# The levels of a gated linear attention: their multiplications all on VectorE, and dense projections set between their products

## The chip, the cores and the metric

The kernel runs on one core of one Trainium2 chip. Its engines work side by side, each through a queue of its own in order: TensorE (PE, matrix products into PSUM), VectorE (DVE), ScalarE (ACT), GpSimd (POOL, which works on SBUF only) and SyncE (SP), which issues the DMAs. The metric is the device time of one execution in microseconds. A shorter time is better. The kernel before takes 3704.74 us, the median of three runs (3701.15 to 3706.63).

## The reference

Two layers of a hybrid transformer over 1024 latent tokens and 256 context tokens, width 1024, in fp32. Each layer has one input projection whose columns are split among three head groups (a 2-D neighbourhood attention, a bidirectional gated linear attention, and a grouped-query attention), one output projection, and a SwiGLU feed-forward block. What the change touches is the projection of the neighbourhood attention's queries and keys, and the part of the linear attention inside its chunks of 64 tokens. The reference computes that part for one direction as

```python
b = jnp.cumsum(gi, axis=-2)
diff = b[..., :, None, :] - b[..., None, :, :]
decay = jnp.exp(jnp.where(causal[:, :, None], diff, -jnp.inf))
A = jnp.einsum('bhtd,bhsd,bhtsd->bhts', qi, ki, decay)
o = jnp.einsum('bhts,bhsv->bhtv', A, vi) + jnp.einsum('bhtd,bhdv->bhtv', qi * jnp.exp(b), S)
```

so that each pair of tokens (t, s) of a chunk has its own decay, the product of all gates between s and t, for each of 32 channels.

## The kernel before

**Layout.** Activations lie with features on the 128 partitions and tokens along the free dimension: 1280 columns, 1024 latent and 256 context. A dense projection is computed with split operands. Each fp32 value is a rounded high part and the rest as a low part, and a product is three matrix products (high x high, high x low, low x high). `mm3` issues them: 8 slices of the inner dimension x 3 = 24 products of up to 512 columns. That is one **chunk**. `wunit` fetches a weight block of 1024 x 128 (a DMA on SP, L238), casts it to its high part on ACT (whi, L249) and subtracts for the low part, here on POOL (wlo, L252). `dense` runs one such block over the token ranges (512, 512 and 256 columns in the first layer and for the keys; the second layer's queries have the two 512 only) and hands each chunk's PSUM bank to an evacuation function. `dense_g` and `products_g` are the same as generators, one chunk per step.

**The linear attention's levels.** The decays inside a chunk of 64 tokens are built in six levels, by doubling. At level `lev` two halves of w = 2^lev tokens meet. Four arrays of 128 x 1280 hold the running decay products: `Fd` and `Hd` (both called dec in the profile; they come from the gates by ACT's exponentials) and `Gd` and `Jd` (which begin as ones). At each level (L603 to L624):
- DVE multiplies the queries with Fd or Hd into X (L609, two halves), POOL the keys with Gd and Jd into xk (L610, L611);
- PE multiplies xk with X in small tiles (`a_mm`, L586: 32 rows, 64 x 64 results) into one of two PSUM buffers called aps. A call is for one of two head pairs and up to eight groups of 128 tokens. The second layer has 8 groups, so two calls a level; the first has 10, so four, two with eight groups and two with two;
- DVE copies the result under the level's mask into A (copy_predicated, L614);
- the four decay arrays are brought to the next level (L621 on DVE, L622 to L624 on POOL).

Ahead of the levels stands one more product without decay, whose diagonal goes into A (L597).

**The neighbourhood projections.** Behind the levels in program order stand six `dense` calls (L638 to L640): for each of three blocks the keys (3 chunks) and the queries (3 chunks in the first layer, 2 in the second), 18 and 15 chunks. `put` evacuates a chunk: ACT scales it into sphi (L630), DVE computes the low part splo (L631), and SP stores both (L633, L634). Behind them come the projection of the linear attention's values, the scan over its states on DVE (L735), and the other projections, woven with the output of the linear attention (L743 and on).

**What sets the order.** The order in each engine's queue is fixed when the kernel is built, by a planner that goes by program order and by its own estimate of when an instruction's operands are there. It may put a chunk between the levels' products where it expects PE to be free. `gate(ins, after)` adds an order between two instructions of one engine without a wait on the chip; `in_order` chains a list of them.

**The modulation's weights.** In the first layer the products with `w_ada` for the later parts are made on DVE (`ada_step`, L177 and L179), 64 steps of two instructions with a weight tile from a DMA each. `ada_later` queues them; every chunk calls `ada_tick(pace["steps"])`, which runs the steps whose weights were fetched at the tick before and fetches for the next ones. Every eight steps two small products with ones add up the sums (L185).

Of the kernel before, what the change touches and what calls it, by code (L numbers as in the profile page):

```python
# [9 lines left out]
F32R = mybir.dt.float32r  # L10
U32 = mybir.dt.uint32
I32 = mybir.dt.int32
AF = mybir.ActivationFunctionType
ALU = mybir.AluOpType
# [5 lines left out]
P = 128  # L20
# [12 lines left out]
FULL = ((0, 512), (512, 512), (1024, 256))  # L33
# [13 lines left out]
W_NQ, W_NK, W_NV, W_LV, W_LQ, W_LK, W_LG, W_LR, W_GQ, W_GK, NW = (  # L47
    0, 384, 768, 1280, 1536, 1664, 1792, 2048, 2080, 2464, 2592)
# [5 lines left out]
def body(ctx: ExitStack, tc, xT, cT, w_ada, w_in, nbias, wa2, w_out, w_fi, w_fo, vecs, cc, consts, ropes, gmask, out):  # L54
    nc = tc.nc
    act, dve, pool, pe = nc.scalar, nc.vector, nc.gpsimd, nc.tensor
# [3 lines left out]
    tmp = ctx.enter_context(tc.tile_pool(name="tmp", bufs=5))  # L60
# [12 lines left out]
    def slot(dt=F32, name="sl"):  # L73
        return slots.tile([P, NT], dt, tag="s", name=name)
# [4 lines left out]
    def bank_q(name):  # L79
        return ps_q.tile([P, 512], F32, tag="q", name=name)  # L80
# [7 lines left out]
    def banks2(pool_, tag, name):  # L88

        return pool_.tile([P, 2, 512], F32, tag=tag, name=name)  # L90
# [4 lines left out]
    def f(ap):  # L95
        return ap.bitcast(F32)
# [68 lines left out]
    ada_todo, ada_run, ada_st = [], [], {}  # L165
# [96 lines left out]
    def mm3(ps, wh, wl, xh, xl, t0, n, c0, cn, natural=False, ks=None):  # L262
        nk = len(xh)
        o = ps[:cn, :n]
        if natural and t0 < SEQ:

            def pick(t):
                return t[:, 0:SEQ].rearrange("p (g r c) -> p r g c", g=8, r=16)[:, t0 // 64:(t0 + n) // 64]
            o = o.rearrange("p (r g c) -> p r g c", g=8, c=8)
        else:  # L270
            def pick(t):
                return t[:, t0:t0 + n]
        for k in ks or range(nk):
            a, b = wh(k, c0, cn), wl(k, c0, cn)
            r, q = pick(xh[k]), pick(xl[k])
            for lhs, rhs, st in ((a, r, k == 0), (a, q, False), (b, r, False)):
                ins = pe.matmul(o, lhsT=lhs, rhs=rhs, start=st, stop=(k == nk - 1 and lhs is b))  # L277
                slip(ins, n, st or (ks and k == ks[0] and rhs is r and lhs is a))
        ada_st["after"] = ins
        return ins  # L280


    hooks = []
# [2 lines left out]
    def slip(ins, n, first):  # L286

        if not hooks:
            return
        if first and hk["last"] is not None:  # L290
            gate(ins, hk["last"])
        hk["c"] += n
        while hooks and hooks[0][0] <= hk["c"]:
            gate(ins, hooks.pop(0)[1])
        hk["last"] = ins if hooks else None
# [5 lines left out]
    pace = {"n": 0, "every": 1, "steps": 1, "w": 0, "lo": 0}  # L301

    def dense(src, xh, xl, tcs, evac, cols=P, natural=False):
        wh, wl = wunit(src, len(xh), cols)
        products(wh, wl, xh, xl, tcs, evac, cols, natural)
# [8 lines left out]
    def run(g):  # L314
        for _ in g:
            pass

    def products(*args):
        run(products_g(*args))

    def dense_g(src, xh, xl, tcs, evac, cols=P, natural=False):
        wh, wl = wunit(src, len(xh), cols)
        yield from products_g(wh, wl, xh, xl, tcs, evac, cols, natural)
# [110 lines left out]
    def gate(ins, after):  # L434

        if after is not None:
            tc.add_manual_dep(ins.ins, after.ins.name, NOSYNC, reason="buffers in order of use")
        return ins

    def in_order(inss):  # L440

        for a, b in zip(inss, inss[1:]):
            gate(b, a)
        return inss[-1]
# [66 lines left out]
    S_NK, S_NQ, S_GQ, S_GK = 0, 3, 6, 9  # L511
    sp = [[dram.tile([2, P, NT], F32, name=f"sp{l}_{i}") for i in range(10)] for l in range(NL)]
# [4 lines left out]
    uh = [slot(F32R, f"uh{k}") for k in range(KT)]  # L517
    ul = [slot(F32R, f"ul{k}") for k in range(KT)]
# [6 lines left out]
    for l in range(NL):  # L525
        last = l == NL - 1
        V = vec[l]
        TOK = LAT if last else FULL
        CT = ((1024, 256),)

        def win(c0, n):
            return w_in[l, :, c0:c0 + n]
# [28 lines left out]
        for e in range(2):  # L561
            ba = V[:, V_BA + e:V_BA + e + 1]
            for (t0, n) in FULL:
                ps = bank_q("zps")
# [4 lines left out]
        ins = [act.activation(a, a, AF.Exp, scale=-1.0) for a in dec][-1]  # L569
        ins = [gate(act.activation(a, a, AF.Ln, bias=one1), ins) for a in dec][-1]  # L570
# [8 lines left out]
        NG = NQ // P  # L579
# [3 lines left out]
        def a_mm(p, ga, gb, xk_, X):  # L583

            ps = banks2(ps_s, "s", "aps")
            in_order([pe.matmul(ps[64 * c:64 * c + 64, hh, (g - ga) * 64:(g - ga + 1) * 64],  # L586
                                lhsT=xk_[32 * (2 * p + hh):32 * (2 * p + hh) + 32, P * g + 64 * c:P * g + 64 * c + 64],
                                rhs=X[32 * (2 * p + hh):32 * (2 * p + hh) + 32, P * g + 64 * c:P * g + 64 * c + 64],
                                start=True, stop=True)
                      for g in range(ga, gb) for c in range(2) for hh in range(2)])  # L590
            return (A[p][:, ga:gb].rearrange("p g h t -> p h g t"),
                    ps[:, :, :(gb - ga) * 64].rearrange("p h (g t) -> p h g t", t=64), gb - ga)

        abanks = [(p, g, min(g + 8, NG)) for g in range(0, NG, 8) for p in range(2)]
        for p, ga, gb in abanks:
            dst, src, n = a_mm(p, ga, gb, gk, gq)
            dve.tensor_tensor(out=dst, in0=src, in1=diag2.unsqueeze(1).unsqueeze(1).to_broadcast([P, 2, n, 64]),  # L597
                              op=ALU.mult)

        def hv(t, n, w):  # L600
            return t[:, :n].rearrange("p (b s w) -> p b s w", s=2, w=w)

        for lev in range(6):  # L603
            w = 1 << lev
            xk_, X = slot(F32, "xk2"), slot(F32, "X")
            g4, j4 = hv(Gd, NQ, w), hv(Jd, NQ, w)
            k4, xk4, q4, X4 = hv(gk, NQ, w), hv(xk_, NQ, w), hv(gq, NQ, w), hv(X, NQ, w)
            for s, dec_ in ((1, Fd), (0, Hd)):
                dve.tensor_tensor(out=X4[:, :, s], in0=q4[:, :, s], in1=hv(dec_, NQ, w)[:, :, s], op=ALU.mult)  # L609
            pool.tensor_tensor(out=xk4[:, :, 0], in0=k4[:, :, 0], in1=g4[:, :, 0], op=ALU.mult)  # L610
            pool.tensor_tensor(out=xk4[:, :, 1], in0=k4[:, :, 1], in1=j4[:, :, 1], op=ALU.mult)  # L611
            for p, ga, gb in abanks:
                dst, src, n = a_mm(p, ga, gb, xk_, X)
                dve.copy_predicated(dst, gm[:, lev].unsqueeze(1).unsqueeze(1).to_broadcast([P, 2, n, 64]), src)  # L614
            f4, h4, g4, j4 = hv(Fd, NT, w), hv(Hd, NT, w), hv(Gd, NT, w), hv(Jd, NT, w)
            nb = NT // (2 * w)

            def bc(ap):
                return ap.to_broadcast([P, nb, w])

            dve.tensor_tensor(out=g4[:, :, 0], in0=g4[:, :, 0], in1=bc(f4[:, :, 1, w - 1:w]), op=ALU.mult)  # L621
            pool.tensor_tensor(out=j4[:, :, 1], in0=j4[:, :, 1], in1=bc(h4[:, :, 0, 0:1]), op=ALU.mult)  # L622
            pool.tensor_tensor(out=f4[:, :, 1], in0=f4[:, :, 1], in1=bc(f4[:, :, 0, w - 1:w]), op=ALU.mult)
            pool.tensor_tensor(out=h4[:, :, 0], in0=h4[:, :, 0], in1=bc(h4[:, :, 1, 0:1]), op=ALU.mult)  # L624


        def put(i, t0, n, src, scale=1.0):
            hi = tmp.tile([P, 512], F32R, tag="t5", name="sphi")
            lo = tmp.tile([P, 512], F32R, tag="t5", name="splo")
            act.activation(hi[:, :n], src, AF.Copy, scale=scale)  # L630
            dve.scalar_tensor_tensor(out=lo[:, :n], in0=src, scalar=scale, in1=f(hi[:, :n]),  # L631
                                     op0=ALU.mult, op1=ALU.subtract)
            nc.sync.dma_start(sp[l][i][0, :, t0:t0 + n], f(hi[:, :n]))  # L633
            nc.sync.dma_start(sp[l][i][1, :, t0:t0 + n], f(lo[:, :n]))  # L634

        if l == 0:
            ada_later(0, (2, 4, 3, 5))
        for i in range(3):  # L638
            dense(win(W_NK + i * P, P), uh, ul, FULL, lambda ps, t0, n, _, i=i: put(S_NK + i, t0, n, ps[:, :n], 0.125))
            dense(win(W_NQ + i * P, P), uh, ul, TOK, lambda ps, t0, n, _, i=i: put(S_NQ + i, t0, n, ps[:, :n]))  # L640

        def v_unit(c0, dst):

# [57 lines left out]
        for p in range(2):  # L701
# [28 lines left out]
            for i in range(1, NCH - 1):  # L730
                for e in range(2):
                    c, nx = order[e][i], order[e][i + 1]
# [3 lines left out]
                                             op0=ALU.mult, op1=ALU.add)  # L736
# [389 lines left out]
        for x, i in enumerate(PAIRS):  # L1126
# [12 lines left out]
            n = done = 0  # L1139
# [42 lines left out]
        first = [(m, w, t0, n, bank_q("mmps")) for m, w in enumerate(wo) for i, (t0, n) in enumerate(LAT)]  # L1182
# [36 lines left out]
        for nh in HCH:  # L1219
            hs = [(slot(F32R, "hh"), slot(F32R, "hl")) for _ in range(nh)]  # L1220
            hh, hl = [h_[0] for h_ in hs], [h_[1] for h_ in hs]
# [19 lines left out]
        if not last:  # L1241
            ada_flush()
            modvec(l + 1, 0, V_L2G, V_L2B, l)
            uh, ul = u2h, u2l
# [117 lines left out]
```

## Time and profile before

| | before |
|---|---|
| median of three runs | 3704.74 us |
| profiled execution | 3701.86 us, span 3700.1 us |
| mean granted TensorE clock | 0.955 |
| TensorE busy | 3423.4 us (93%) |
| VectorE busy | 1634.0 us (44%) |
| GpSimd busy | 1243.6 us (34%) |
| ScalarE busy | 920.2 us (25%) |
| levels of the first layer | about 106 to 199 us |
| levels of the second layer | about 2110 to 2178 us |

All lines come from one profiled execution. A line of the timeline has the start in us from the span's beginning, the duration in us, the engine, the line of the kernel, the operation, what it writes and reads, the shape and how many instructions are merged; in brackets stands how long the engine was idle before it, and what ended that. A line of the groups has the busy time, the mean duration in ns, and the idle time before with its releasers. A granted clock of 1.00 is full speed.

### The profile page before, as it was taken

How to read it: one execution, taken by the hardware profiler on the slowest of the kernel's cores; microseconds unless marked ns; L12 is line 12 of the kernel's file. 1: busy time of each engine (PE TensorE's matmuls, PEld its weight loads, DVE VectorE, ACT ScalarE, POOL GpSimd, SP SyncE). 2: the span in 40 equal slices, each digit the busy share in tenths (PEclk: the TensorE clock that was granted, in tenths of full speed). 3: DMA queues.
4: the chain of work that ended last, by engine and by line, in shares of the span. 5: the costliest groups of instructions: out<-in, count | busy, mean ns of one | idle time of the engine just before them, and what ended most of it. 6: DMA issues, size and time to landing. Idle time of an engine off the chain costs nothing.

```text
span 3700.1 us, 49312 instructions
## 1 busy us (share of the span) xinstructions
PE 3423.4 (93%) x20832; PEld 2536.6 (69%) x20832; DVE 1634.0 (44%) x2475; ACT 920.2 (25%) x1365; POOL 1243.6 (34%) x747
## 2 busy tenths in 40 slices
PE   6698997889999999999999969998889999999998
PEld 3587873434678888888876657783335688888875
DVE  3757555553444554454235553325552532222233
ACT  2213212333231111111114403212332311111113
POOL 1712304664451111111125552324663622222222
PEclk8799998999999999999999979998999999999998
DMA  5152240102221222221123212121103111111122
GB/s 174 42 159 78 96 178 20 63 1 79 70 60 63 90 84 74 75 94 61 35 74 95 72 58 72 60 106 46 58 1 103 49 43 56 47 47 52 47 72 85
DMA packets 287276, 262.93 MB, mean 71 GB/s; under 512 B 13840, under 2 KB 238416, under 8 KB 287056
## 3 DMA queue, kind: packets, MB, share of 16 engines
q1 hardware_dynamic: 287056, 259.80, 22.0%
q8 instruction: 163, 2.67, 0.3%
q14 instruction: 57, 0.47, 0.0%
HBM read 226.72 MB, written 33.03 MB: 70 GB/s over the span
## 4 chain that ended last, share of the span: by engine, by line
PE 81%; DVE 11%; ACT 4%; issue 2%; POOL 2%; DMA 1%; SPq 0%; ACTq 0%; DVEq 0%; POOLq 0%
PE mmps L277 60%; PE sT L476 4%; PE vps L656 3%; DVE m L935 3%; PE fs L358 2%; PE gav L951 2%; PE gs L484 2%; DVE S L735 1%; ACT gpt L1055 1%; DVE ut L229 1%; DVE slat L918 1%; PE nmT L459 1%; DVE ptl L1024 1%; PE spr L429 1%; PE adaps L185 1%
## 5 line engine op out<-in xcount | busy, mean ns | idle before, releaser
L252 POOL TENSOR_TENSOR wlo<-wraw,whi 128x1024 fp32r<-128x1024 f32 (+3 forms) x228 | 503.2, 2209 | 1770.5 <-ACT whi L249 1708.8
L277 PE MATMUL mmps<-oh,whi 128*128 128x512 f32 (+2 forms) x2416 | 905.8, 376 | 13.1 <-ACT whi L249 7.1
L277 PE MATMUL mmps<-oh,wlo 128*128 128x512 f32 (+1 forms) x2416 | 903.2, 374 | 2.6 <-POOL wlo L252 2.5
L277 PE MATMUL mmps<-ol,whi 128*128 128x512 f32 (+1 forms) x2416 | 902.5, 374 | 1.9 <-DVE ol L231 1.9
L277 PEld LDWEIGHTS mmps<-oh,whi 128*128 128x128 f32 (+1 forms) x2416 | 457.6, 189 | 122.5 <-issue 20.3
L277 PEld LDWEIGHTS mmps<-oh,wlo 128*128 128x128 f32 x2416 | 457.0, 189 | 114.5 <-issue 24.7
L277 PEld LDWEIGHTS mmps<-ol,whi 128*128 128x128 f32 x2416 | 457.5, 189 | 97.3 <-issue 16.6
L249 ACT CAST whi<-wraw 128x1024 fp32r<-128x1024 f32 (+3 forms) x262 | 251.8, 962 | 964.6 <-PE mmps L277 907.8
L1207 DVE TENSOR_TENSOR sg<-mmps,sg 128x512 f32<-128x512 f32 (+1 forms) x110 | 70.1, 637 | 603.0 <-PE mmps L277 598.7
L277 PE MATMUL mmps<-hl,whi 128*128 128x512 f32 (+1 forms) x880 | 324.8, 370 | 1.0 <-DVE hl L1209 1.0
L277 PE MATMUL mmps<-hh,whi 128*128 128x512 f32 (+1 forms) x880 | 324.1, 371 | 0.0
L277 PE MATMUL mmps<-hh,wlo 128*128 128x512 f32 (+1 forms) x880 | 321.2, 369 | 0.0
L1176 DVE SCALAR_TENSOR_TENSOR z<-mmps,mod,z 128x512 f32<-128x512 f32 (+1 forms) x320 | 217.8, 694 | 198.4 <-PE mmps L277 197.6
L179 DVE SCALAR_TENSOR_TENSOR adacc<-adaw,scc,adacc 128x512 f32<-128x512 f32 x280 | 239.2, 897 | 92.8 <-DMA adaw<-in_w_ada_dram 92.3
L1047 POOL TENSOR_TENSOR gacc<-gacc,gpt 128x1024 f32<-128x1024 f32 x80 | 189.9, 2375 | 80.7 <-ACT gpt L1055 80.5
L935 DVE TENSOR_REDUCE m<-gs 128x2 f32<-128x1024 f32 (+1 forms) x150 | 154.8, 1032 | 107.6 <-PE gs L484 107.6
L277 PEld LDWEIGHTS mmps<-hh,whi 128*128 128x128 f32 x880 | 165.9, 189 | 41.3 <-issue 9.2
L277 PEld LDWEIGHTS mmps<-hh,wlo 128*128 128x128 f32 x880 | 165.6, 189 | 31.9 <-issue 2.5
L277 PEld LDWEIGHTS mmps<-hl,whi 128*128 128x128 f32 x880 | 166.2, 189 | 30.1 <-DVE hl L1209 1.2
L277 PE MATMUL mmps<-uh,whi 128*128 128x512 f32 (+3 forms) x408 | 155.6, 388 | 28.4 <-ACT uh L230 18.8
L1055 ACT ACTIVATE gpt<-sT 128x1024 f32<-128x1024 f32 x120 | 122.9, 1024 | 182.2 <-PE sT L476 166.9
L1209 DVE TENSOR_TENSOR hl<-sg,hh 128x512 fp32r<-128x512 f32 (+1 forms) x110 | 128.7, 1170 | 67.1 <-ACT hh L1208 67.1
(238 smaller groups left out, 4636.7 us busy)
## 6 DMA issues: line engine op xcount, KB each, us to landing
wraw<-in_w_fi_dram SPq DMA_DIRECT2D x106, 512.0 KB, 3.9
adaw<-in_w_ada_dram SPq DMA_DIRECT2D x160, 256.0 KB, 3.6
wraw<-in_w_fo_dram SPq DMA_DIRECT2D x60, 384.0 KB, 3.1
wraw<-in_w_in_dram SPq DMA_DIRECT2D x40, 512.0 KB, 3.9
wraw<-in_w_out_dram SPq DMA_DIRECT2D x36, 512.0 KB, 3.6
sp<-sphi SPq DMA_DIRECT2D x40, 256.0 KB, 2.0
sp<-splo SPq DMA_DIRECT2D x40, 256.0 KB, 2.1
adaw<-in_w_ada_dram SPq DMA_DIRECT2D x16, 512.0 KB, 7.3
```

Source lines behind the costliest of these rows:

```text
L179: dve.scalar_tensor_tensor(out=a, in0=raw, scalar=scc[:, k, s_:s_ + 1], in1=a, op0=ALU.mult, op1=ALU.add)
L249: act.copy(a[:, :m], rw)
L252: (dve if pace["lo"] and pace["w"] % pace["lo"] == 0 else pool).tensor_tensor(out=b[:, :m], in0=rw, in1=f(a[:, :m]), op=ALU.subtract)
L277: ins = pe.matmul(o, lhsT=lhs, rhs=rhs, start=st, stop=(k == nk - 1 and lhs is b))
L358: ins = pe.matmul(ps[32 * q:32 * q + 32, :n], lhsT=ones[:, 0:32], rhs=src(kt), start=(kt < 4), stop=(kt >= 4))
L476: inss = [pe.matmul(ps[:, e, :n], lhsT=w[rows(e), c0:c0 + P], rhs=m[rows(e), q0:q0 + n], start=(i == 0), stop=(i == 3)) for i, (w, m, c0) ...
L656: ins = pe.matmul(ps[:, :256], lhsT=lhs, rhs=rhs, start=(k == 0 and i == 0), stop=(k == KT - 1 and i == 2))
L935: dve.tensor_reduce(out=m3[:, j, :, c], in_=ps[:, :, :n], axis=AX.X, op=ALU.max)
L1047: (dve if q and i == 5 else pool).tensor_tensor(out=acc[q], in0=prev if kb == 1 else acc[q], in1=pt, op=ALU.add)
L1055: act.activation(pt, ps, AF.Exp)
L1176: dve.scalar_tensor_tensor(out=zz, in0=ps[:, :n], scalar=g[:, m + c, s:s + 1], in1=zz, op0=ALU.mult, op1=ALU.add)
L1209: dve.tensor_tensor(out=b_[:, sl], in0=sg[:, sl], in1=f(a_[:, sl]), op=ALU.subtract)
```

## The change

- The five multiplications of a level that POOL made (xk twice, and Jd, Fd, Hd) are made by DVE.
- The six projections become one generator, `na_units`, made ahead of the levels. In each level, after the masked copy of the second head pair, the kernel takes chunks from it: two in the second layer, and in the first one after each of the two pairs of calls. So 12 of 18 and 12 of 15 chunks are taken inside the levels; the rest run behind them.
- PE's order inside is written out: with `fill["on"]` the first product of a chunk is ordered behind the last small product or chunk before it, and the small products behind the last chunk.
- The first layer's modulation steps are still queued behind the levels, but now run two a chunk in place of one.

```diff
+        first = fill["on"]
         for k in ks or range(nk):
...
                 ins = pe.matmul(o, lhsT=lhs, rhs=rhs, start=st, stop=(k == nk - 1 and lhs is b))
+                if first:
+                    gate(ins, fill["last"])
+                    first = False
                 slip(ins, n, st or (ks and k == ks[0] and rhs is r and lhs is a))
-        ada_st["after"] = ins
+        ada_st["after"] = fill["last"] = ins
         return ins
+    fill = {"on": False, "last": None}
...
-            in_order([pe.matmul(ps[64 * c:64 * c + 64, hh, (g - ga) * 64:(g - ga + 1) * 64],
+            inss = ([pe.matmul(ps[64 * c:64 * c + 64, hh, (g - ga) * 64:(g - ga + 1) * 64],
...
+            if fill["on"]:
+                gate(inss[0], fill["last"])
+            fill["last"] = in_order(inss)
...
+        def na_units():
+            for i in range(3):
+                yield from dense_g(win(W_NK + i * P, P), uh, ul, FULL,
+                                   lambda ps, t0, n, _, i=i: put(S_NK + i, t0, n, ps[:, :n], 0.125))
+                yield from dense_g(win(W_NQ + i * P, P), uh, ul, TOK,
+                                   lambda ps, t0, n, _, i=i: put(S_NQ + i, t0, n, ps[:, :n]))
+
+        na_chunks = na_units()
...
-            pool.tensor_tensor(out=xk4[:, :, 0], in0=k4[:, :, 0], in1=g4[:, :, 0], op=ALU.mult)
-            pool.tensor_tensor(out=xk4[:, :, 1], in0=k4[:, :, 1], in1=j4[:, :, 1], op=ALU.mult)
+            dve.tensor_tensor(out=xk4[:, :, 0], in0=k4[:, :, 0], in1=g4[:, :, 0], op=ALU.mult)
+            dve.tensor_tensor(out=xk4[:, :, 1], in0=k4[:, :, 1], in1=j4[:, :, 1], op=ALU.mult)
             for p, ga, gb in abanks:
                 dst, src, n = a_mm(p, ga, gb, xk_, X)
                 dve.copy_predicated(dst, gm[:, lev].unsqueeze(1).unsqueeze(1).to_broadcast([P, 2, n, 64]), src)
+                if p == 1:
+                    fill["on"] = True
+                    for _ in range(2 if NG == 8 else 1):
+                        next(na_chunks)
...
-            pool.tensor_tensor(out=j4[:, :, 1], in0=j4[:, :, 1], in1=bc(h4[:, :, 0, 0:1]), op=ALU.mult)
-            pool.tensor_tensor(out=f4[:, :, 1], in0=f4[:, :, 1], in1=bc(f4[:, :, 0, w - 1:w]), op=ALU.mult)
-            pool.tensor_tensor(out=h4[:, :, 0], in0=h4[:, :, 0], in1=bc(h4[:, :, 1, 0:1]), op=ALU.mult)
+            dve.tensor_tensor(out=j4[:, :, 1], in0=j4[:, :, 1], in1=bc(h4[:, :, 0, 0:1]), op=ALU.mult)
+            dve.tensor_tensor(out=f4[:, :, 1], in0=f4[:, :, 1], in1=bc(f4[:, :, 0, w - 1:w]), op=ALU.mult)
+            dve.tensor_tensor(out=h4[:, :, 0], in0=h4[:, :, 0], in1=bc(h4[:, :, 1, 0:1]), op=ALU.mult)
+
+        fill["on"] = False
         if l == 0:
             ada_later(0, (2, 4, 3, 5))
-        for i in range(3):
-            dense(win(W_NK + i * P, P), uh, ul, FULL, lambda ps, t0, n, _, i=i: put(S_NK + i, t0, n, ps[:, :n], 0.125))
-            dense(win(W_NQ + i * P, P), uh, ul, TOK, lambda ps, t0, n, _, i=i: put(S_NQ + i, t0, n, ps[:, :n]))
+            pace.update(every=1, steps=2)
+        run(na_chunks)
```

More of the change, by code (lines that the diff above doesn't have):

```diff
@@ L589, in a_mm, with put @@
                                 start=True, stop=True)
-                      for g in range(ga, gb) for c in range(2) for hh in range(2)])
+                     for g in range(ga, gb) for c in range(2) for hh in range(2)])
+            if fill["on"]:
+                gate(inss[0], fill["last"])
+            fill["last"] = in_order(inss)
             return (A[p][:, ga:gb].rearrange("p g h t -> p h g t"),
                     ps[:, :, :(gb - ga) * 64].rearrange("p h (g t) -> p h g t", t=64), gb - ga)
+        def put(i, t0, n, src, scale=1.0):
+            hi = tmp.tile([P, 512], F32R, tag="t5", name="sphi")
+            lo = tmp.tile([P, 512], F32R, tag="t5", name="splo")
+            act.activation(hi[:, :n], src, AF.Copy, scale=scale)
+            dve.scalar_tensor_tensor(out=lo[:, :n], in0=src, scalar=scale, in1=f(hi[:, :n]),
+                                     op0=ALU.mult, op1=ALU.subtract)
+            nc.sync.dma_start(sp[l][i][0, :, t0:t0 + n], f(hi[:, :n]))
+            nc.sync.dma_start(sp[l][i][1, :, t0:t0 + n], f(lo[:, :n]))
+        def na_units():
[5 more added lines that the diff above has]
+        na_chunks = na_units()
         abanks = [(p, g, min(g + 8, NG)) for g in range(0, NG, 8) for p in range(2)]
@@ L621, in body @@
             dve.tensor_tensor(out=g4[:, :, 0], in0=g4[:, :, 0], in1=bc(f4[:, :, 1, w - 1:w]), op=ALU.mult)
-            pool.tensor_tensor(out=j4[:, :, 1], in0=j4[:, :, 1], in1=bc(h4[:, :, 0, 0:1]), op=ALU.mult)
-            pool.tensor_tensor(out=f4[:, :, 1], in0=f4[:, :, 1], in1=bc(f4[:, :, 0, w - 1:w]), op=ALU.mult)
-            pool.tensor_tensor(out=h4[:, :, 0], in0=h4[:, :, 0], in1=bc(h4[:, :, 1, 0:1]), op=ALU.mult)
[L627 to L634, printed above, removed]
+            dve.tensor_tensor(out=j4[:, :, 1], in0=j4[:, :, 1], in1=bc(h4[:, :, 0, 0:1]), op=ALU.mult)
+            dve.tensor_tensor(out=f4[:, :, 1], in0=f4[:, :, 1], in1=bc(f4[:, :, 0, w - 1:w]), op=ALU.mult)
+            dve.tensor_tensor(out=h4[:, :, 0], in0=h4[:, :, 0], in1=bc(h4[:, :, 1, 0:1]), op=ALU.mult)
+        fill["on"] = False
         if l == 0:
             ada_later(0, (2, 4, 3, 5))
-        for i in range(3):
-            dense(win(W_NK + i * P, P), uh, ul, FULL, lambda ps, t0, n, _, i=i: put(S_NK + i, t0, n, ps[:, :n], 0.125))
-            dense(win(W_NQ + i * P, P), uh, ul, TOK, lambda ps, t0, n, _, i=i: put(S_NQ + i, t0, n, ps[:, :n]))
+            pace.update(every=1, steps=2)
+        run(na_chunks)
         def v_unit(c0, dst):
```

## The prediction

> **What bounds the kernel now.** I read the page first (busy shares, chain), then the busy time of the engines in the stage that is edited, in both layers, then the groups and the order of instructions there.
>
> ```profile
> span 3700.1 us, 49312 instructions
> PE 3423.4 (93%) x20832; PEld 2536.6 (69%) x20832; DVE 1634.0 (44%) x2475; ACT 920.2 (25%) x1365; POOL 1243.6 (34%) x747
> PE 81%; DVE 11%; ACT 4%; issue 2%; POOL 2%; DMA 1%; SPq 0%; ACTq 0%; DVEq 0%; POOLq 0%
> ```
>
> TensorE (PE) sets the end: 93% busy, 81% of the chain of waits. So time is to be had only where PE stands still or runs at a low clock. The stage of the levels is such a place. The columns of the next view are the stretch, then the busy time of PE, weight loads, DVE, ACT and POOL, the granted clock and the DMA share:
>
> ```profile
> 106.30:199.00 92.70, 60.20 (x1105) 49.30 (x1101) 74.71 (x65) 12.06 (x13) 57.51 (x33) 0.72 0.12 39
> 2113.00:2178.00 65.00, 28.68 (x800) 25.15 (x799) 55.70 (x38) 5.82 (x6) 49.84 (x30) 0.61 0.03 10
> ```
>
> PE idles 32.5 us in the first layer's stage and 36.3 us in the second's, and what it does there it does at clocks of 0.72 and 0.61. DVE (81% and 86%) and POOL (62% and 77%) are the busy ones. Their operations, by groups, second layer (busy, mean ns, idle before):
>
> ```profile
> L586 PE MATMUL aps<-X,xk 32*64 32x64 f32 x768 | 21.2, 297 | 36.3 <-DVE A L614 28.6 <-POOL dec L623 6.6 <-DVE X L609 1.0
> L609 DVE TENSOR_TENSOR X<-gq,dec 128x512 f32<-128x512 f32 x12 | 18.4, 1531 | 4.6 <-POOL dec L623 4.0 <-ACT dec L573 0.4
> L614 DVE COPY_PREDICATED A<-gm,aps 128x1024 f32<-128x1024 uint32 x12 | 15.7, 1316 | 1.7 <-PE aps L586 1.6
> L621 DVE TENSOR_TENSOR Gd<-Gd,dec 128x640 f32<-128x640 f32 x6 | 12.4, 2070 | 1.2 <-POOL xk L610 1.2
> L611 POOL TENSOR_TENSOR xk<-gk,Jd 128x512 f32<-128x512 f32 x6 | 10.7, 1780 | 0.0
> L623 POOL TENSOR_TENSOR dec<-dec 128x640 f32<-128x640 f32 x6 | 9.5, 1584 | 2.3 <-DVE Gd L621 2.3
> ```
>
> The level's products wait 28.6 us for DVE's masked copy (L614), which stands late in DVE's queue because DVE's own multiplications take 1.53 to 2.07 us each. Single instructions show why (start, duration):
>
> ```profile
> 118.14 0.81 DVE L621 TENSOR_TENSOR Gd<-Gd,dec 128x640 f32<-128x640 f32 x1
> 119.03 1.25 POOL L623 TENSOR_TENSOR dec<-dec 128x640 f32<-128x640 f32 x1 [1.83 <-DVE Gd L621]
> 2129.77 1.83 POOL L622 TENSOR_TENSOR Jd<-Jd,dec 128x640 f32<-128x640 f32 x1
> 2129.85 2.31 DVE L609 TENSOR_TENSOR X<-gq,dec 128x512 f32<-128x512 f32 x1
> 2152.64 0.68 DVE L609 TENSOR_TENSOR X<-gq,dec 128x512 f32<-128x512 f32 x1
> 136.34 0.43 DVE L614 COPY_PREDICATED A<-gm,aps 128x256 f32<-128x256 uint32 x1
> 2124.48 0.68 DVE L631 SCALAR_TENSOR_TENSOR splo<-mmps,sphi 128x512 fp32r<-128x512 f32 x1
> ```
>
> A multiplication that starts beside one of POOL takes 2.31 us; one that runs by itself 0.68 (512 columns) or 0.81 (640). The 0.81 is at level 0, where every operand is strided, so stride is no reason to expect more.
>
> **The change part by part.** (1) Five POOL multiplications a level (L610, L611, L622 to L624) become DVE's. A level then has eight on DVE: first layer 8 x 0.81 = 6.5 us, second 4 x 0.68 + 4 x 0.81 = 6.0. With the masked copies (2 x 1.32 + 2 x 0.43 = 3.5; 2 x 1.32 = 2.6) and two chunks' splo (1.2 and 1.3, as some chunks have 256 columns) DVE needs 11.2 and 9.9 us a level. The bounds of one multiplication are 0.68 and the contended mean of 2.07; I take the uncontended rows, since POOL keeps only the split of the weights.
>
> (2) Twelve of the 18 (15) chunks move between the levels' products, in a fixed PE order. A chunk's price, from the ACT copies that end each (512, 256 and 512 columns):
>
> ```profile
> 222.05 0.60 ACT L630 ACTIVATE sphi<-mmps 128x512 fp32r<-128x512 f32 x1 [4.21 <-PE mmps L277]
> 227.49 0.60 ACT L630 ACTIVATE sphi<-mmps 128x512 fp32r<-128x512 f32 x1 [4.84 <-PE mmps L277]
> 235.83 0.60 ACT L630 ACTIVATE sphi<-mmps 128x512 fp32r<-128x512 f32 x1 [4.20 <-PE mmps L277]
> 256.26 0.60 ACT L630 ACTIVATE sphi<-mmps 128x512 fp32r<-128x512 f32 x1 [5.04 <-PE mmps L277]
> ...
> 2240.24 0.60 ACT L630 ACTIVATE sphi<-mmps 128x512 fp32r<-128x512 f32 x1 [4.21 <-PE mmps L277]
> ```
>
> 512 columns: 227.49 - 222.05 = 5.44; the next two, 256 and 512: 8.34, so 256 columns cost 2.90 and a unit of three 13.78. Before, the last projection ends on PE at 256.26 + 2.90 = 259.2 in the first layer and at 2240.24 + 5.44 = 2245.7 in the second. PE is bound to this stage from here on:
>
> ```profile
> 106.30 0.80 PE L277 MATMUL mmps<-uh,whi 128*128 128x512 f32 x1
> 118.36 1.98 PE L586 MATMUL aps<-X,xk 32*64 32x64 f32 x64 [3.05 <-DVE A L597]
> 164.92 2.21 PE L586 MATMUL aps<-X,xk 32*64 32x64 f32 x160
> ...
> 2110.08 0.80 PE L277 MATMUL mmps<-oh,whi 128*128 128x512 f32 x1
> 2110.68 0.63 PE L277 MATMUL mmps<-ol,whi 128*128 128x512 f32 x1
> 2111.10 0.63 PE L277 MATMUL mmps<-oh,wlo 128*128 128x512 f32 x1
> ...
> 2117.64 0.39 PE L277 MATMUL mmps<-oh,wlo 128*128 128x512 f32 x1
> 2117.86 0.39 PE L277 MATMUL mmps<-oh,whi 128*128 128x512 f32 x1
> 2119.24 1.99 PE L586 MATMUL aps<-X,xk 32*64 32x64 f32 x128 [0.99 <-DVE X L609]
> ...
> 2172.40 5.42 PE L586 MATMUL aps<-X,xk 32*64 32x64 f32 x192 [2.30 <-DVE A L614]
> 2177.76 0.80 PE L277 MATMUL mmps<-oh,whi 128*128 128x512 f32 x1
> ```
>
> The chunk that now fills 106.3 and 2110.1 may no longer run there: the first one is gated behind level 0, which waits for ACT's exponentials. So PE stands from 106.3 to 118.3 (12.0 us) and from 2110.1 to about 2119.3 (9.2 us); I keep today's starts, as level 0's extra multiplications fit into DVE's wait for ACT. A level's small products cost 2.0 us warm for 128 instructions (2119.24), so 2.0 in the second layer and 160 x 15.5 ns = 2.5 in the first (164.92 says 2.2). Cold, 192 take 5.42 us, so 128 take 3.6, and the first eight dense products stand 0.42 apart instead of 0.22 (2110.68 to 2111.10 against 2117.64 to 2117.86): 1.6 + 1.6, rounded with the larger first layer to 3.6 a layer for a cold start.
>
> The Trainium skill (TensorE: Matmul & The Clock Gate, "Part 1: The HAM clock gate") says that any 3.4 us of sustained work bring full clock back. By it the small products alone would warm PE and the cold start would cost about 2 instead of 3.6. The trace disagrees: after 5.4 us of small products the dense ones at 2177.76 still start at half rate.
>
> PE per level is then (4 x 13.78)/6 + 2.5 = 11.7 us in the first layer and (10 x 5.44 + 2 x 2.90)/6 + 2.0 = 12.0 in the second, DVE 11.2 and 9.9: PE is the bound, closely in the first. Sums from PE's start to the last projection:
> first layer: before 259.2 - 106.3 = 152.9; after 12.0 + 55.1 + 6 x 2.5 + 3.6 + 27.6 (six chunks left) + 2 (small products of the modulation) = 115.3. Gain 37.6.
> second: before 2245.7 - 2110.1 = 135.6; after 9.2 + 60.2 + 6 x 2.0 + 3.6 + 13.8 (three left) = 98.8. Gain 36.8.
> Against the 74.4 I set 6 us of gaps (0.5 a level, where DVE meets the weights' split or a short chunk pair).
>
> (3) The weights' split (wlo, POOL, 2.35 us a unit) is no longer behind POOL's multiplications; it is hidden under a unit of 13.8 us. ACT (12.06 us busy in the stage) and SP have room for the sphi copies, the weight loads and the stores that now come earlier. If a load came late, its whole delay would stand on PE.
>
> (4) In the first layer the modulation's steps start after the levels, two a chunk. Rows: PE and DVE in the stretches behind, then the steps (L179) alone.
>
> ```profile
> 300.00:340.00 40.00, 29.56 (x240) 24.79 (x240) 33.95 (x88) 15.86 (x40) 2.56 (x3) 0.79 0.19 63
> 340.00:460.00 120.00, 120.00 (x894) 97.96 (x893) 66.28 (x133) 32.41 (x58) 36.77 (x23) 0.97 0.28 93
> 340.00:460.00 120.00, 24.33 (x25) 0.97 0.28 93
> 460.00:545.00 85.00, 28.65 (x38) 0.97 0.51 178
> 324.94 3.45 DVE L179 SCALAR_TENSOR_TENSOR adacc<-adaw,scc,adacc 128x512 f32<-128x512 f32 x2
> 331.30 0.79 PE L277 MATMUL mmps<-uh,whi 128*128 128x512 f32 x1 [6.70 <-DVE ms L421]
> ```
>
> DVE's total is the same, but 340 to 460 carries up to 24 us more (66 to 90 of 120), and what stood at 460 to 545 goes. PE already lost 6.70 us behind two such steps, which sit ahead of the copy it needs. One more pair there costs up to 3.45, and the end of the stage gives some back: I take a loss of 4, between a gain of 5 and a loss of 12.
>
> Sum: 74.4 - 6 - 4 = 64.4 us off the profiled execution's 3701.9, which is 3637. The median of the runs is 3704.7, 0.08% more; I forecast 3637.
>
> **Rivals.** (a) DVE becomes the bound. At 1.25 us a multiplication (halfway) a level costs 14.7 and 13.9 us, 18 + 11 us over PE: about 3637 - 6 + 29 = 3660; at today's mean of 1.8 (19.1 and 18.3 us a level) 82 us over, 3713. For it: every long row of DVE; against it: those have a POOL row beside them, and POOL now has nine wlo in both stages together. The Trainium skill (SBUF — State Buffer, "Summary: rules for kernel authors") says that the later of two such instructions is blocked until the first ends; by it each wlo would hold DVE for up to 2.35 us, 9.4 us in the first layer, of which 6 would pass on to PE, my 6 us again.
> (b) Slower: the second chunk's splo stands ahead of the next level's multiplications in DVE's queue. Then after that chunk PE waits 0.6 (sphi) + 0.68 + 4 x 0.68 to 0.81, about 4.3 us, and restarts cold (3.6): 7.9 a level, 95 for twelve, 3637 - 6 + 95 = 3726. From nine such levels on it beats the gain. For it: today's queue put masked copies late in just this way. Against: the multiplications need nothing of the second chunk, and DVE is free for them during its 5.4 us.
> (c) The gain is given back behind the stage in the first layer (scan and modulation steps, the 12 us bound and another 6 for the scan): 3650 to 3660.
> (d) The change doesn't fill PE, because weights come late: if both stages keep their length, 3702.
>
> **Chances.** Forecast 0.70 (own range 3620 to 3650), (a) 0.10, (b) 0.05, (c) 0.11, (d) 0.04. The range 3615 to 3672 holds the forecast, (c) and the half price of (a). A difference under 0.2% (7 us) can't be told from none. Faster 0.92; within 0.2% 0.04, from (d) and the dear end of (a) in part; slower 0.04, from (b).
>
> **What would show it.** Right: PE nearly full from level 0 to the last projection, at clock 1.0; DVE multiplications of 0.7 to 0.8 us; the last projection about 38 us sooner in each layer, relative to the stage's start. Step 1 falls if those multiplications stay above 1.2 us; step 2 if PE waits over 1 us at each level for X or xk; step 4 if PE idles much over 10 us in the scan's stretch of the first layer. The forecast is wrong if both stages shorten and the end doesn't follow.

## The result, and the profile after

The changed kernel takes 3658.69 us, the median of four runs (3657.83 to 3662.02), where the kernel before takes 3704.28 in the same comparison. The ratio is 0.9881, with a 95% interval of 0.9869 to 0.9894: 45.6 us less. The forecast was 68 us less than the median of before. The time lies inside the whole range of 3615 to 3672, but above the forecast's own 3620 to 3650. It is in the range of rival (c), though (c)'s mechanism isn't what the profile shows: that the two agree is chance.

The head of the profile after, then the two stages from PE's start to its last projection (stretch, length, busy time of PE, weight loads, DVE, ACT and POOL, granted clock, DMA share, GB/s):

```profile
span 3656.3 us, 49289 instructions
PE 3406.7 (93%) x20832; PEld 2519.1 (69%) x20832; DVE 1640.7 (45%) x2535; ACT 920.8 (25%) x1365; POOL 1150.5 (31%) x687
...
109.10:241.60 132.50, 110.05 (x1397) 91.03 (x1398) 92.61 (x118) 20.95 (x29) 19.52 (x7) 0.87 0.32 98
2097.40:2204.80 107.40, 92.44 (x1133) 78.71 (x1130) 67.58 (x82) 20.69 (x27) 23.37 (x7) 0.89 0.27 87
```

The same two stretches of the kernel before:

```profile
106.30:259.20 152.90, 120.40 (x1423) 99.66 (x1420) 103.73 (x105) 22.76 (x30) 68.05 (x37) 0.83 0.30 95
2110.10:2245.70 135.60, 99.28 (x1133) 84.78 (x1130) 65.15 (x52) 20.77 (x27) 62.62 (x36) 0.79 0.21 69
```

The stages are 20.4 and 28.2 us shorter, where 37.6 and 36.8 were forecast. POOL is busy for 19.5 and 23.4 us of them, where it was for 68.1 and 62.6. But PE still stands for 22.5 and 15.0 us, and its clock is 0.87 and 0.89, not 1.0. Groups of the second layer's stage after (busy, mean ns, idle before) show where the gain came from:

```profile
L593 PE MATMUL aps<-X,xk 32*64 32x64 f32 x768 | 13.3, 235 | 9.7 <-DVE X L637 9.7
L637 DVE TENSOR_TENSOR X<-gq,dec 128x512 f32<-128x512 f32 x12 | 8.1, 689 | 0.0
L654 DVE TENSOR_TENSOR Jd<-Jd,dec 128x640 f32<-128x640 f32 x6 | 5.0, 834 | 0.0
```

Here the level's products no longer wait 28.6 us for the masked copy; what is left is the wait ahead of level 0. A multiplication into X takes 0.69 us where it took 1.53, and Jd 0.83 where POOL took 1.61 on average.

What PE waits for in the first layer's stage and, behind the dots, in the second's (us in all, times, longest):

```profile
PE aps L593 <- DVE X L637: 10.1, 1, 10.1
PE aps L593 <- DVE A L642: 5.3, 2, 4.8
PE mmps L278 <- DVE A L642: 5.1, 1, 5.1
PE mmps L278 <- DVE splo L609: 1.9, 1, 1.9
...
PE aps L593 <- DVE X L637: 9.7, 1, 9.7
PE mmps L278 <- DVE splo L609: 5.3, 2, 3.4
```

The waits for X are level 0's. The others are new. A dense chunk (mmps) needs nothing of the masked copy (A) or of an earlier chunk's splo, except that they read the PSUM bank that it is to write. The longest of these in the second layer, first on ACT and DVE, then on PE:

```profile
2117.60 0.60 ACT L608 ACTIVATE sphi<-mmps 128x512 fp32r<-128x512 f32 x1 [12.12 <-PE mmps L278]
...
2118.81 1.35 DVE L642 COPY_PREDICATED A<-gm,aps 128x1024 f32<-128x1024 uint32 x1
...
2126.86 0.82 DVE L655 TENSOR_TENSOR dec<-dec 128x640 f32<-128x640 f32 x1
2127.59 0.69 DVE L609 SCALAR_TENSOR_TENSOR splo<-mmps,sphi 128x512 fp32r<-128x512 f32 x1
...
2128.33 0.58 PE L278 MATMUL mmps<-oh,whi 128*128 128x256 f32 x1 [3.40 <-DVE splo L609]
```

The first chunk's sphi is done at 2118.2. Its splo runs only at 2127.59, because a masked copy and, behind it, eleven multiplications for later levels stand ahead of it in DVE's queue. The third chunk, at 2128.33, waits for just this splo, so it was given the first chunk's bank. PE then restarts at half rate: its products of 256 columns stand 0.21 us apart, and the granted clock is 0.50 from 2128.3 to 2134.0.

The third kind of wait, in the first layer's level 5, on POOL, DVE and PE:

```profile
168.59 3.39 POOL L710 TENSOR_TENSOR Gd<-Gd,gk 128x1280 f32<-128x1280 f32 x1 [14.53 <-DVE Gd L653]
169.10 3.56 DVE L655 TENSOR_TENSOR dec<-dec 128x640 f32<-128x640 f32 x1
171.94 2.98 POOL L252 TENSOR_TENSOR wlo<-wraw,whi 128x1024 fp32r<-128x1024 f32 x1
172.58 3.01 DVE L656 TENSOR_TENSOR dec<-dec 128x640 f32<-128x640 f32 x1
174.87 3.46 POOL L711 TENSOR_TENSOR Jd<-Jd,gk 128x1280 f32<-128x1280 f32 x1
175.85 3.08 DVE L708 COPY gtot<-dec 64x20 f32<-64x20 f32 x4
178.96 2.80 DVE L642 COPY_PREDICATED A<-gm,aps 128x1024 f32<-128x1024 uint32 x3
180.30 0.70 PE L593 MATMUL aps<-X,xk 32*64 32x64 f32 x16 [4.78 <-DVE A L642]
```

POOL still has two multiplications behind the levels (L710 and L711, Gd and Jd by the keys) and the weights' split. Each of the two DVE multiplications begun beside one of POOL's instructions ends about 0.7 us after it, the copies into gtot are held by L711 in the same way, and the masked copy behind them comes so late that PE waits 4.8 us. By the Trainium skill (SBUF — State Buffer, "Summary: rules for kernel authors") the later of the two is blocked until the first ends; these rows agree: POOL's first ends at 168.59 + 3.39 = 171.98, DVE's at 172.66, and the 0.68 between them is near the 0.82 that such a multiplication takes by itself (2126.86 above).

### The profile page after: what moved, and what is told of

It reads as the page before. It is cut to its first block, busy times and chain, and to the rows that moved or that the text cites. A ratio compares the mean times of both kernels' runs of the same rounds, so it can differ in the third digit from the quotient of the medians.

```text
span 3656.3 us, 49289 instructions
## 1 busy us (share of the span) xinstructions
PE 3406.7 (93%) x20832; PEld 2519.1 (69%) x20832; DVE 1640.7 (45%) x2535; ACT 920.8 (25%) x1365; POOL 1150.5 (31%) x687
## 5 line engine op out<-in xcount | busy, mean ns | idle before, releaser
L278 PE MATMUL mmps<-uh,whi 128*128 128x512 f32 (+3 forms) x408 | 155.1, 387 | 25.8 <-ACT uh L230 18.8
```

## The experiments

"Against the change" below is a kernel's median less 3658.69. All were measured against the kernel before on the chip that they ran on, and intervals are 95%.

**The two halves alone.** mult_only is the kernel before with the multiplications on DVE; fill_only is the changed kernel with them on POOL.

```diff
 (mult_only, for each of the five; fill_only the reverse)
-            pool.tensor_tensor(out=j4[:, :, 1], ...
+            dve.tensor_tensor(out=j4[:, :, 1], ...
```

> The kernel before, with the five POOL multiplications of each level on DVE and nothing else: projections behind the levels as before, modulation steps one a chunk. Theory (the filling is the gain, the multiplications only let it): DVE multiplications of 0.68 to 0.82 us, the levels some 5 to 15 us shorter a layer, PE still idle for most of them; 3680 to 3695. Rival (most of the gain is in taking the multiplications off POOL): 3660 to 3668.

> The changed kernel with the five multiplications left on POOL; the twelve chunks a layer stand between the products as in the changed kernel. Theory: DVE's multiplications stay at 1.5 to 2 us, the weights' split waits behind POOL's multiplications, so PE waits at each level for X, xk or weights; about half of the gain, 3675 to 3690. Rival (the order on PE alone brings it): within 3 us of the changed kernel's 3659.

mult_only: 3676.09 us, ratio 0.9925 (0.9908 to 0.9942), 27 less than before, between what the theory and its rival expected. fill_only: 3672.87, ratio 0.9915 (0.9900 to 0.9929), 30 less, a little better than expected. The longest waits of PE in the second layer's stage, of mult_only and then of fill_only with one of its groups:

```profile
PE aps L586 <- DVE A L614: 18.5, 5, 12.4
```

```profile
PE mmps L278 <- DVE splo L609: 12.1, 2, 7.1
PE aps L593 <- DVE X L637: 8.9, 1, 8.9
...
L637 DVE TENSOR_TENSOR X<-gq,dec 128x512 f32<-128x512 f32 x12 | 18.7, 1562 | 11.0 <-POOL dec L655 8.7 <-POOL dec L656 1.9 <-ACT dec L580 0.4
```

Each half gains by itself; 27 and 30 make 57, the whole 46, so they overlap. The profiles show where. In the first layer fill_only's stage takes 132.4 us (109.3 to 241.7), as long as the change's 132.5: there the move of the multiplications adds nothing to the filling. In the second layer it takes 116.1 us (2098.5 to 2214.6) against 107.4. And the waits that fill_only's theory named, for X, xk or weights at each level, are not the longest: beside level 0's it is splo, that is, banks. In fill_only X takes 1562 ns where it takes 689 in the change, with only the engine of five other multiplications changed, so the contention between DVE and POOL is shown, not only argued.

**The banks.** In banks4 the chunks inside the levels take four PSUM buffers by turns; in the change the planner chooses a bank, and in the second layer's levels it used two.

```diff
+        fill["banks"] = [ps_q.tile([P, 512], F32, tag="fq", name="fq", bufs=4) for _ in range(4)]
         for lev in range(6):
...
-                ps = bank_q("mmps")
+                if fill["on"]:
+                    fill["n"] += 1
+                    ps = fill["banks"][fill["n"] % 4]
+                else:
+                    ps = bank_q("mmps")
```

> The changed kernel, with four PSUM banks set aside for the filled chunks and used by turns, where the planner gave them two or three. Theory (in the levels PE waits for banks whose last reader, splo, stands in DVE's queue behind multiplications; waits of 5.1 and 1.9 us in the first layer, 3.4 and 1.9 in the second, each long one followed by a cold start of about 3): the waits go, 3642 to 3650. Rival (DVE as a whole is the bound in the levels, the wait only moves to the masked copies or to X): 3655 to 3660.

3644.82 us, ratio 0.9840 (0.9825 to 0.9854), 13.9 less than the change. The second layer's stage in banks4, and PE's only wait in it:

```profile
2094.30:2194.40 100.10, 90.43 (x1129) 76.53 (x1130) 67.44 (x81) 20.68 (x27) 20.53 (x7) 0.92 0.29 93
...
PE aps L597 <- DVE X L642: 9.7, 1, 9.7
```

The stage is 100.1 us instead of 107.4, 1.3 from the 98.8 of the prediction's sum without gaps. The waits for splo are gone. So for the second layer the bank is shown as their cause. The total meets the expectation in part by luck, though. From the last of these projections to the second layer's first value product banks4 takes 160.8 us and the change 169.6: 8.8 of the gain lie where nothing was edited. There a wait of PE for DVE (ms, in the next projections) falls from 6.4 to 1.6 us, as the planner ordered that place anew. In the first layer the stage hardly moved, 131.9 against 132.5 us. PE's waits there in banks4, beside 10.1 us for level 0 (`fq` is the name of the four banks):

```profile
PE aps L597 <- DVE A L647: 7.0, 4, 4.8
PE fq L278 <- DVE A L647: 2.8, 1, 2.8
```

The wait for splo is gone there too, and the first chunk's is 2.8 instead of 5.1, but the small products' waits for masked copies grew from 5.3 to 7.0. In this layer the rival came in part: some of the waiting moved to the masked copies.

**Level 0's wait.** In early one chunk of the projections is made ahead of level 0, where PE waits 10 us.

```diff
+        next(na_chunks)
+
         def hv(t, n, w):
```

> The changed kernel, with one chunk a layer taken ahead of level 0, so that it may run while ACT makes the exponentials (one less is left behind the levels). Theory (of the changed kernel's two standstills before level 0, 10.1 and 9.7 us, a chunk of 5.44 us fits into each, cold some 7): up to 11 us less, 3648 to 3652. Rival (what it fills is lost again at level 0, since DVE's multiplications or the cold clock set that start): 3656 to 3660.

3646.84 us, ratio 0.9844 (0.9831 to 0.9858), 11.9 less than the change and slightly better than expected. The wait, in the second layer:

```profile
PE aps L593 <- DVE X L639: 5.9, 1, 5.9
```

It falls by 3.8 us there, and in the first layer's stage no wait of over 3.3 is left. The wait for level 0 was time that the change had emptied, and a chunk fits into it. In the profile the last of the projections comes 8.1 us sooner than in the change in the first layer, and in the second layer's stage 3.2 are gained. What lies between loses some 8, and behind the second layer's projections 7 are gained (162.5 us to the first value product, 169.6 in the change), both where nothing was edited. The edited places make 11.3, and that the total of 11.9 is so near is luck in part, here too.

**The tail of level 5.** tail makes the two last multiplications by gk on DVE, behind the last masked copy, and orders the four small copies into gtot there too.

```diff
-                dve.copy_predicated(dst, gm[:, lev]...
+                lastcp = dve.copy_predicated(dst, gm[:, lev]...
...
-                dve.tensor_copy(tot[p][d_], ...)
+                gate(dve.tensor_copy(tot[p][d_], ...), lastcp)
...
-        pool.tensor_tensor(out=Gd, in0=Gd, in1=gk, op=ALU.mult)
-        pool.tensor_tensor(out=Jd, in0=Jd, in1=gk, op=ALU.mult)
+        gate(dve.tensor_tensor(out=Gd, in0=Gd, in1=gk, op=ALU.mult), lastcp)
+        gate(dve.tensor_tensor(out=Jd, in0=Jd, in1=gk, op=ALU.mult), lastcp)
```

> The changed kernel, with the copies to gtot behind the last masked copy of the levels in DVE's queue, and the two long multiplications of Gd and Jd by the keys (POOL, 128 x 1280) on DVE, behind it too. Theory (these two POOL instructions run beside the last levels' DVE work and draw it out: 3.56 and 3.01 us for two multiplications, 8.26 for four small copies; PE waits 4.8 us in the first layer and 1.9 in the second for it, and starts cold once): 6 to 9 us less, 3650 to 3653. Rival (the waits come from DVE's total, the moved work is late for the scan instead): 3657 to 3661.

3653.08 us, ratio 0.9862 (0.9848 to 0.9875), 5.6 less than the change, just short of the expected 6 to 9. The two intervals overlap, so the total alone doesn't show a gain. The profile does: the late masked copy's wait of 4.8 is gone, and the stages are 4.1 and 3.0 us shorter than in the change. The small copies of tail in the second layer, as a group:

```profile
L708 DVE COPY gtot<-dec 64x20 f32<-64x20 f32 x4 | 0.7, 175 | 0.0
```

**The modulation's steps.** step1 puts them back to one a chunk; step12 uses one a chunk up to the value projections and two from there on.

```diff
 (step1)
-            pace.update(every=1, steps=2)
+            pace.update(every=1, steps=1)
 (step12, beside it)
+        if l == 0:
+            pace.update(steps=2)
         weave(units[6:], starts(), 3, 1)
```

> The changed kernel, with the modulation's steps at one a chunk behind the levels in place of two. Theory (behind the first layer's levels PE waits 20 us at the small products L185 for the steps on DVE, against 1.4 before): that wait falls under 6 us, of which the steps left over for the end of the stage take some back; 3648 to 3656. Rival (the scan on DVE sets the pace there whatever the steps): 3657 to 3661, or slower by the steps left over.

> The changed kernel, with the modulation's steps at one a chunk from the levels to the gates' projections, and two a chunk only in the two value projections at the end of the stage, so that none are left over. Theory (two a chunk delays the scan's stretch by some 15 us, one a chunk leaves steps over that hold up the first attention pairs; both go): the value projections begin at 434 us as with one a chunk, the first scores by 520; 3645 to 3650. Rival (the maxima of the first pair share DVE with the value projections, and two steps a chunk hold them up there): 3660 to 3672.

Both theories fell; both times are where the rivals put them. step1: 3672.09 us, ratio 0.9914 (0.9899 to 0.9929), 13.4 more than the change. step12: 3662.90, ratio 0.9890 (0.9876 to 0.9903), 4.2 more, which its interval doesn't tell from the change. In the change PE's wait at L185 was 10.6 us, not the 20 of step1's theory; in step1 it is 5.8. What was expected at the front did happen: the value projections (vps) begin at 434.0 us in step1 and 434.9 in step12, against 449.1 in the change. Then most of it is lost again. From the start of the last value product to the first attention scores (sT) it takes 4.5 us in the change, 15.6 in step1 and 16.5 in step12. The last steps on DVE in this stretch, of the change, step1 and step12:

```profile
457.59 1.41 DVE L179 SCALAR_TENSOR_TENSOR adacc<-adaw,scc,adacc 128x512 f32<-128x512 f32 x2 [1.43 <-DMA adaw<-in_w_ada_dram]
```

```profile
540.75 1.41 DVE L179 SCALAR_TENSOR_TENSOR adacc<-adaw,scc,adacc 128x512 f32<-128x512 f32 x2 [1.25 <-DMA adaw<-in_w_ada_dram]
```

```profile
526.00 1.41 DVE L179 SCALAR_TENSOR_TENSOR adacc<-adaw,scc,adacc 128x512 f32<-128x512 f32 x2
```

In the change the steps end 71 us before the first scores, at 530.3. In the other two they run up to them (533.2 in step12) or past them (528.6 in step1). Step1 is thus still 1.7 us ahead at the first scores, and 6.8 behind at the first pair's first value products (cav, 547.9 against 541.1), with the last steps in between. The rest of its 13.4 comes later, where nothing was edited. Step12's stretch from the value products to the first scores (columns as in the first windows) has PE idle for half of it and at a low clock, and the DMA queues are busy for 0.72 of it:

```profile
516.70:533.20 16.50, 7.62 (x28) 3.85 (x27) 11.78 (x27) 0.96 (x2) 0.00 (x0) 0.67 0.72 265
```

In the stretch from the last projection to these scores, PE's waits for the maxima on DVE (mx and mc) are 2.8 us in the change, 7.5 in step1 and 7.8 in step12, as the rival of step12 expected. Whether DVE's steps or the transfers of their weights hold them up was not separated.

**All together.** combo joins banks4, early, tail and step12. combo2 joins the first three and keeps two steps a chunk.

```diff
 (combo: the edits of banks4, early, tail and step12)
 (combo2: the edits of banks4, early and tail)
```

> Four banks by turns, one chunk ahead of level 0, the long multiplications and gtot copies behind the last masked copy on DVE, and the modulation's steps one a chunk, two in the value projections. Theory (the four losses are separate): about 14 + 9 + 7 + 10 us less than the changed kernel, 3615 to 3630. Rival (they overlap, since one late chain on DVE is behind all): 3636 to 3645.

> The changed kernel with the four banks by turns, the chunk ahead of level 0 and the tail on DVE together, and the modulation steps as the change has them, two a chunk. Alone the three edits took 13.9, 11.9 and 5.6 us off the changed kernel's 3658.7. If the three waits are separate places on PE, and the steps at two a chunk are the better choice because what they delay ahead of the value projections is had back behind them, the sum is 3627 (3624 to 3632), and below the combination with the steps at one and two. If the edits overlap (the early chunk also takes away a wait for a bank in level 0), 3633 to 3640, no better than that combination's 3633.9.

combo: 3633.85 us, ratio 0.9812 (0.9798 to 0.9825), 24.8 less than the change and the fastest kernel of this study, between its two expectations. combo2: 3642.18, ratio 0.9835 (0.9822 to 0.9849). Its own expectation of a plain sum (3627) fell, it lies above the 3633 to 3640 of overlapping edits too, and its median is 8.3 above combo's although step12 alone had been slower than the change. The two intervals just overlap, and the two profiled executions are only 2.7 us apart. In the profiles combo2 leads up to the end of the first layer: its last product of the feed-forward block there starts at 1973.52 us, against 1977.18 in combo and 1989.53 in the change. From there to the second layer's first value product, where the two have the same text, combo2 takes 381.8 us and combo 375.4. PE's wait at level 0 in that stretch, of combo2, then of combo:

```profile
PE aps L597 <- DVE X L644: 5.9, 1, 5.9
```

```profile
PE aps L597 <- DVE X L644: 2.8, 1, 2.8
```

From the last of the projections to that product both take what the change takes (169.9 and 169.7 us), so the 8.8 us of banks4 are not among what can be added up. In the first layer the edits do add up: the last projection's sphi begins 0.8 us sooner than in the change in banks4, 8.1 in early and 5.1 in tail, which make 14.0, and 16.4 in combo. The planner orders the whole layer anew with each edit: places that no edit touched moved by 6 to 9 us. Why the order of the second layer differs between the two combinations was not settled. The four runs of combo lie between 3629.8 and 3639.3, the profiled one at 3637.8.

## Why the prediction was right or wrong

**The direction and its causes: right.** Step 1 held in the second layer (0.69 and 0.83 us against 0.68 and 0.81). In the first, five of the eight groups of multiplications have means of 0.82 us, and three of 1.10 to 1.28 (xk at L638, and dec at L655 and L656), as single ones stand beside POOL. So rival (a), with 1.25 for all of them, didn't come. Step 2's pieces held: the wait ahead of level 0 was 10.1 and 9.7 us (12.0 and 9.2 predicted), the second layer's small products took 13.3 us (six levels of 2.0 and 1.6 for the cold start make 13.6), and no level but the first waited for X or xk. Of (c), which gave back 13 to 23 us more behind the first layer's stage, 0.9 came. Of (b) the place was right and the order the reverse, as the next part shows. (d) didn't come: no wait in the stages is for weights.

**The term that failed: "6 us of gaps (0.5 a level)".** The stages were to be 115.3 and 98.8 us without gaps, and were 132.5 and 107.4: gaps of 17.2 and 8.6, 25.8 in all. The windows split them. PE's idle time is 22.5 and 15.0 against the 12.0 and 9.2 set down for level 0, which is 10.5 and 5.8 more: new waits of 12.3 and 5.3, while level 0's came out 1.9 shorter and 0.5 longer. PE's busy time is 110.1 and 92.4 against 103.3 and 89.6. Most of these 6.8 and 2.8 can be read as products at the lower clock behind such waits (0.50 for 5.7 us behind the one of 3.4); no experiment separates them. The prediction looked for late operands (X, xk, the weights' split) and set 0.5 us a level on them. What came were PSUM banks that DVE read late, in three places: the first layer's first chunk behind a masked copy (5.1), chunks behind a splo in DVE's queue (1.9 and 5.3), and the first layer's level 5, where POOL's L710 and L711 hold up DVE (4.8). It asked what stood queued behind a splo, in rival (b), and not what a splo stood behind. Its sentence that POOL keeps only the split of the weights overlooked the two multiplications behind the levels (of POOL's seven instructions in each stage five are wlo, ten in all and not nine).

banks4 took the second layer's gaps from 8.6 to 1.3 and left the first layer's; tail took 4.1 off the first layer's stage. For the rest of the first layer's 17.2 no single experiment accounts, and its cause stays open beyond what PE's waits name.

**Step (4), a loss of 4 behind the first stage: right in size.** From the last projection to the first scores:

```profile
259.20:543.10 283.90, 268.34 (x2123) 222.51 (x2121) 174.34 (x343) 71.17 (x148) 61.98 (x37) 0.95 0.34 114
```

```profile
241.50:530.30 288.80, 271.83 (x2130) 223.12 (x2129) 184.43 (x363) 71.75 (x149) 60.55 (x37) 0.95 0.35 112
...
PE adaps L185 <- DVE adacc L179: 10.6, 4, 4.7
```

Before (the first fence) it took 283.9 us, after 288.8: a loss of 4.9. The waits for the steps (10.6) replace a 6.7 of before. But that one step a chunk would save this time, as step1's theory had it, is refuted: that kernel is 13.4 slower.

**The balance.** The profiled executions are 3701.86 and 3658.13 us, 43.7 apart, against 64.4 predicted. Gaps took 19.8 more than the 6 set down; the first stage starts 2.8 us later (109.1 against 106.3); the loss behind it is 4.9, not 4; and 2.8 more were gained behind the second stage. 64.4 - 19.8 - 2.8 - 0.9 + 2.8 = 43.7.

## What to carry to other kernels

When dense work is set into another chain's gaps, price the PSUM banks and not the operands alone: for each bank, ask which instruction frees it, and what stands ahead of that one in its engine's queue. A queue whose engine isn't the bound runs ahead in its own order, and may put work that nobody waits for in front of the evacuation that PE needs: here eleven multiplications, and 3.4 us of PE. Judge a background job's pace by where it ends as well as by where it runs: here the pace that delayed the value projections by 15 us was the better one. Its steps were over 71 us before the first scores, while those of the slower pace ran past them; what exactly they hold up there stays open.

## What the runs showed of the hardware

**Small copies beside POOL.** The four copies into gtot (64 x 20 elements) take 175 ns each in tail, where POOL is idle. In the changed kernel they lie beside POOL's multiplications:

```profile
2145.31 4.94 POOL L710 TENSOR_TENSOR Gd<-Gd,gk 128x1280 f32<-128x1280 f32 x1 [4.49 <-DVE Gd L653]
2150.22 2.93 POOL L711 TENSOR_TENSOR Jd<-Jd,gk 128x1280 f32<-128x1280 f32 x1
2153.11 2.34 POOL L252 TENSOR_TENSOR wlo<-wraw,whi 128x1024 fp32r<-128x1024 f32 x1
...
2147.23 8.26 DVE L708 COPY gtot<-dec 64x20 f32<-64x20 f32 x4
```

They take 8.26 us together, twelve times as long, and end at 2155.49, with POOL's third instruction (2153.11 + 2.34 = 2155.45). So a tiny copy can pay for a whole POOL instruction. It seems to go the other way too: L710 begins among DVE's multiplications and takes 4.94 us, where L711, with only a copy beside it, takes 2.93.

**Small products let the clock fall.** From combo2, PE between two dense chunks of the second layer (`zps`, and the `aps` between its rows, have 32 rows):

```profile
2078.09 0.28 PE L278 MATMUL mmps<-ol,whi 128*128 128x256 f32 x1
2078.20 0.28 PE L278 MATMUL mmps<-oh,wlo 128*128 128x256 f32 x1
2078.41 1.98 PE L576 MATMUL zps<-lrT,wa 32*128 32x512 f32 x4
...
2083.01 2.14 PE L576 MATMUL zps<-lrT,wa 32*128 32x512 f32 x4
2085.08 0.80 PE L278 MATMUL mmps<-oh,whi 128*128 128x512 f32 x1
2085.68 0.63 PE L278 MATMUL mmps<-ol,whi 128*128 128x512 f32 x1
2086.10 0.63 PE L278 MATMUL mmps<-oh,wlo 128*128 128x512 f32 x1
...
2090.74 0.40 PE L278 MATMUL mmps<-ol,whi 128*128 128x512 f32 x1
2090.97 0.40 PE L278 MATMUL mmps<-oh,wlo 128*128 128x512 f32 x1
```

PE has no idle time here. The dense products before stand 0.12 us apart at 256 columns; after 6.7 us of products with 32 rows they stand 0.42 apart at 512, and 0.23 only from 2090.74 on, 5.7 us later. The granted clock is 0.91 from 2078.4 to 2085.1 and 0.50 from 2085.1 to 2090.7. So products with 32 rows didn't keep the clock up here. The Trainium skill (TensorE: Matmul & The Clock Gate, "Part 1: The HAM clock gate") counts a window of time in which PE is busy, about 3.4 us; here PE was busy without a break and came out at half rate, so by this measurement these products don't count as such work.
